# The first mixer's eight leading products, copied out of their banks ahead of the norm's factor

## The chip, the core and the metric

One program on one core of a Trainium2 chip. The metric is the device time of one execution in microseconds (us); the median of several runs is compared. TensorE (PE) multiplies, VectorE (DVE), ScalarE (ACT) and GpSimd (POOL) work on vectors, and SyncE (SP) and ACT issue DMAs.

## What is computed

Two transformer-like blocks, one behind the other, on 512 tokens of width 1024 in fp32. The change lies in the first block's mixer:

```python
u = rms_norm(h, mix_pre_g[l])
proj = u @ w_in[l]
(q_a, k_a, v_a, q_i, k_i, w_i, gate_b, gate_c, conv_in,
 g_a, g_b) = jnp.split(proj, split_points, axis=-1)
...
y_a = dsa_attention(q_a, k_a, v_a, q_i, k_i, w_i) @ w_a_out[l]
z = short_conv_causal(gate_c * conv_in, conv_w[l])
y_b = (gate_b * z) @ w_b_out[l]
merged = jax.nn.sigmoid(g_a) * y_a + jax.nn.sigmoid(g_b) * y_b
h = h + rms_norm(merged @ w_out[l], mix_post_g[l])
```

Ahead of it, `q_a`, `k_a`, `q_i` and `k_i` are rotated (rope). `dsa_attention` is sparse: an indexer sums relu(q_i . k_i) over eight heads with weights w_i into a score for each pair of tokens, a top-k of the scores picks the keys of each query, and the softmax runs over these alone. Memory cross-attention and a gated feed-forward end the first block; the second has a mixer with two attentions, a feed-forward and a gated addition.

## The kernel before

Features lie on the 128 partitions, tokens along the free dimension. A product takes eight slices of the 1024 inputs; each slice is three matmuls of halves in fp32r (`mm3`, L284 to L294), so a product of 128 outputs is 24 matmuls of 512 tokens, or 24 of 256 for half of the tokens (halves A and B). A weight is loaded raw by SP, cast on ACT (L252) and its rest taken on DVE (L253); two raw buffers and five cast pairs take turns.

The norm's factor is a number for each token, so a product can start on the gained input and be multiplied by the factor afterwards. `begin` (L316) uses this: it starts a stage's leading products by halves while the stage before it is still being normed and added. A half's steps come in lists: `post` (the factor of the stage before), `body` (adding, squares L563, the new input and its rest L513 and L514) and `norm` (sums on PE L582, root on DVE, the factor spread by PE L593 and copied by ACT L598). One step is issued behind each product, and what is to be done with a product (`put`) follows once its half's factor is known, which is what keeps the product in its PSUM bank until then. Weights for these products lie in buffers of the kinds that `K['lead:mix']` names (u and b are buffers of activations, w a regular pair).

There are five banks for products: three of the kind `lg`, two of the kind `mm`, taken in turn by a running count (`pm`); once `attending` is set only `mm` is taken, and the count runs on. Small buffers have eight slots (`t`), large ones 32 (`b`).

In the mixer, five leading products are the indexer's key (kk, which also holds the attention's key) and its four query tiles (qi0 to qi3). Their `put` is the rope: four ACT instructions (L785) fetch swapped quarters from the bank into y, DVE multiplies the bank by the cosine into x (L787), POOL multiplies y by the sine (L790), DVE adds (L791). The tables of cosine and sine are scaled by the factor on POOL first (L946). Values and head weights (vw, multiplied by the factor at L930) follow as a product of all tokens by `stream`. Then key and query tiles are split into halves of heads (L802, L803, L812 to L815), 24 pairs of indexer logits run (L823, L824) with a relu on ACT (L980) and a sum on DVE (L981) each, beside them the four query products of the attention (QA); 48 rounds of top-k on DVE (L992, L993), with the twelve convolution products and the first gates on PE beside them; and the attention, whose softmax begins at L833. A convolution step multiplies two products, c and ci, and three taps on them. Every engine works its own list in order; the list follows from the program's order through a scheduling layer, which lets engines run ahead of each other within the limits of buffers.

Of the kernel before, what the change touches and what calls it, by code (L numbers as in the profile page):

```python
# [15 lines left out]
OP = mybir.AluOpType  # L16
# [34 lines left out]
T_KK, T_QI, T_VW, T_QA, T_CONV, T_GB, T_GA = 0, 1, 5, 6, 10, 22, 30  # L51
# [35 lines left out]
 'urg:mixsh': 1,  # L87
 'sq:mixsh': 'PV',
 'bf:mix': [0, 1, 4, 6],
 'lead:mix': 'ubbbb',  # L90
 'ahead:mix': 5,
 'late:mix': [5, 0],
 'urg:crosssf': 1,
# [85 lines left out]
class Net:  # L179
# [123 lines left out]
    def begin(self, jobs, step, fill=()):  # L303


        first, second = step(A), step(B)
        wts = []
        for (w, n, xs, k0, _), tag in zip(jobs, K["lead:" + self.phase]):
            wts.append(self.lead_weights(w, n, len(xs), k0, tag) if tag != "w" else self.weights(w, n, len(xs), k0)[0])
        todo = first["post"] + first["body"] + first["norm"][:1]  # L310
        for go in self.rest:
            if todo:
                todo.pop(0)()
            go()
        self.rest = []
        for do in todo:  # L316
            do()
        todo = (second["post"][:2] + first["norm"][1:2] + second["post"][2:] + first["norm"][2:]
                + second["body"] + second["norm"])

        def advance():
            if todo:
                todo.pop(0)()

        for go in fill:
            go()
            advance()
        for _ in range(3):
            advance()

        for tok, d in zip(HALVES, (first, second)):
            waiting = []
            for (_, _, xs, _, put), wt in zip(jobs, wts):
                waiting.append((put, self.lin(wt, xs, tok)))
                advance()
                if not any(do in todo for do in d["norm"]):
                    while waiting:
                        put, ps = waiting.pop(0)
                        put(ps, tok)
            while any(do in todo for do in d["norm"]):  # L340
                advance()
            for put, ps in waiting:
                put(ps, tok)
        for do in todo:
            do()
# [428 lines left out]
    def rotated(self, w, n, xs, cos, sin, g=None, squares=None):  # L774

        nc = self.nc
        x, y = self.tmp(), self.tmp()

        def put(ps, tok):
            if squares is not None:  # L780
                nc.scalar.activation(squares[:, tok], ps, AF.Square)

            for b in range(4):
                src = slice(32 * (b ^ 1), 32 * (b ^ 1) + 32)
                nc.scalar.activation(y[32 * b : 32 * b + 32, tok], ps[src], AF.Copy, scale=1.0 if g is None else g[src])  # L785
            if g is None:
                nc.vector.tensor_tensor(x[:, tok], ps, cos[:, tok], op=OP.mult)  # L787
            else:
                nc.vector.scalar_tensor_tensor(x[:, tok], ps, g, cos[:, tok], op0=OP.mult, op1=OP.mult)
            nc.gpsimd.tensor_tensor(y[:, tok], y[:, tok], sin[:, tok], op=OP.mult)  # L790
            (nc.gpsimd if self.spared and K["F1"] else nc.vector).tensor_tensor(x[:, tok], x[:, tok], y[:, tok], op=OP.add)  # L791

        return x, (w, n, xs, 0, put)

    def heads(self, x):
# [123 lines left out]
    def projection(self, w, n, xs, r, alloc=None, light=False):  # L919

        nc = self.nc
        t = (alloc or self.tmp)((P, S), F32)

        def put(ps, tok):
            if light:
                nc.scalar.copy(t[:, tok], ps)  # L926
                if r is not None:
                    nc.gpsimd.tensor_tensor(t[:, tok], t[:, tok], r[:, tok], op=OP.mult)  # L928
            else:
                nc.vector.tensor_tensor(t[:, tok], ps, r[:, tok], op=OP.mult)  # L930

        return t, (w, n, xs, 0, put)

    def project(self, *args, **kw):
# [4 lines left out]
    def mix(self):  # L939
        self.phase = "mix"  # L940
        nc, h = self.nc, self.h
        cos, sin, cm = self.table("cos1"), self.table("sin1"), self.table("causal")

        def more(tok, r, rs):
            for t in (cos, sin):
# [2 lines left out]
        xs, r, step = self.enter("mix_pre_g", more)  # L948
        w = "w_in"
        turns = [self.rotated(w, n, xs, cos, sin) for n in (T_KK, T_QI, T_QI + 1, T_QI + 2, T_QI + 3)]  # L950
        vw, last = self.projection(w, T_VW, xs, r)
        self.begin([j for _, j in turns], step)
        self.stream([last])
        self.attending = True
        kk = turns[0][0]
        ka, ki = self.keys(kk, 0), self.keys(kk, 1)
# [5 lines left out]
        for j in range(NT):  # L962
            ps = self.pa()
# [5 lines left out]
        first = self.cp.tile([P, P], F32, tag="first", name="first")  # L969
# [3 lines left out]
        for i in range(1, NT):  # L973
            n = (i + 1) * P
            sc = self.big((P, n), F32)
            for hd in range(H):
                ps = self.bank("lg")
                self.logits(ps, qi[hd], hd % 2, i, ki, n)
                t = self.tmp((P, n))
# [5 lines left out]
        for t in range(4):  # L985
            x, job = self.rotated(w, T_QA + t, xs, cos, sin)
# [13 lines left out]
        rr = self.rowtile()  # L1000
        nc.gpsimd.tensor_tensor(rr, r, r, op=OP.mult)
        for j in range(4):
            c = self.project(w, T_CONV + 3 * j, xs, None, light=True)
            ci = self.project(w, T_CONV + 3 * j + 1, xs, None, light=True)
            nc.gpsimd.tensor_tensor(c, c, ci, op=OP.mult)
            nc.gpsimd.tensor_tensor(c, c, rr, op=OP.mult)
            tap = [self.gains[:, G_CONV + 3 * j + d : G_CONV + 3 * j + d + 1] for d in range(3)]
            z = self.tmp()
            nc.scalar.activation(z, c, AF.Copy, scale=tap[2])
            for d in (1, 0):  # L1010
                s = 2 - d
                nc.vector.scalar_tensor_tensor(z[:, s:], c[:, : S - s], tap[d], z[:, s:], op0=OP.mult, op1=OP.add)
            b = self.project(w, T_CONV + 3 * j + 2, xs, r, light=True)
            nc.gpsimd.tensor_tensor(b, b, z, op=OP.mult)
            bz.append(self.split(b, self.pair()))
# [618 lines left out]
```

## Time and profile before

| what | value |
|---|---|
| median of 3 runs | 2095.18 us (2094.7 to 2096.39) |
| the profiled execution, its own time | 2091.38 us |
| its span | 2089.6 us |
| mean granted clock of PE | 0.99 |
| busy: PE, DVE, ACT, POOL | 2011.4, 1544.4, 1101.7, 254.4 us |

The span is the time from the first instruction to the last in the profile; 1.8 us of the execution lie around it. The profiled execution is 3.8 us under the median. In the rows further down, a timeline's line gives the start, the busy time, engine and line, and what the instruction writes and reads; in square brackets stands how long the engine was idle before and what it waited for. Times are from the start of the span. A granted clock of 1.00 is 2.4 GHz, 0.50 is 1.2 GHz.

### The profile page before, as it was taken

Reading aid. Unit: us, or ns where it says so; the run is one execution under the profiler, and the core shown is the slowest. Engines: PE = TensorE matmul, PEld = TensorE weight load, DVE = VectorE, ACT = ScalarE, POOL = GpSimd, SP = SyncE. Lnnn points to the kernel's source line nnn. Section 1 sums busy time; section 2 is a strip of 40 time slices with the busy share of each in tenths; the row PEclk is TensorE's granted clock in tenths of the full one; section 3 lists DMA queues with packets and bytes.
Section 4 is the critical chain, followed back from the end, with each engine's and each line's share of the span. In section 5 each row is a group of like instructions: output and inputs, shape, how many; then the busy total and the mean of one; then the engine's idle time right before and its main releaser. Section 6 shows DMA issues by size and latency. Waiting matters only on the chain. (4 is left out here: it accounts for less than half of the span.)

```text
span 2089.6 us, 32337 instructions
## 1 busy us (share of the span) xinstructions
PE 2011.4 (96%) x12428; PEld 1766.1 (85%) x12428; DVE 1544.4 (74%) x2956; ACT 1101.7 (53%) x2052; POOL 254.4 (12%) x239
## 2 busy tenths in 40 slices
PE   8999999899999999999999998998999999999997
PEld 7899998778778888998999998776778888988997
DVE  7977786799775585587777869588987678666755
ACT  5644454673573454554445445467864436444752
POOL 2000002313331310040000003213100000000001
PEclk9999999899999999999999999999999999999999
DMA  5233333212222233221333342211112313323331
GB/s 163 91 112 97 106 107 122 71 61 91 91 71 95 77 120 103 93 70 51 113 110 102 106 141 72 66 41 51 41 41 81 114 31 122 99 89 104 112 101 41
DMA packets 66010, 186.43 MB, mean 89 GB/s; under 512 B 6976, under 2 KB 14144, under 8 KB 65856
## 3 DMA queue, kind: packets, MB, share of 16 engines
q1 hardware_dynamic: 63376, 180.97, 26.8%
q10 hardware_dynamic: 2448, 3.41, 0.5%
q8 instruction: 97, 1.59, 0.3%
q14 instruction: 57, 0.47, 0.1%
q0 software_dynamic: 32, 0.00, 0.0%
HBM read 182.25 MB, written 2.10 MB: 88 GB/s over the span
## 5 line engine op out<-in xcount | busy, mean ns | idle before, releaser
L290 PE MATMUL mm<-x,w 128*128 128x512 f32 (+1 forms) x2064 | 473.8, 379 | 0.0
L290 PE MATMUL mm<-b,w 128*128 128x256 f32 (+1 forms) x2625 | 448.6, 322 | 2.0 <-ACT b L510 1.8
L290 PEld LDWEIGHTS mm<-x,w 128*128 128x128 f32 x2064 | 364.0, 188 | 74.9 <-DVE v L1274 0.7
L290 PEld LDWEIGHTS mm<-b,w 128*128 128x128 f32 x2625 | 375.2, 188 | 48.9 <-ACT b L510 4.2
L252 ACT CAST w<-r 128x1024 fp32r<-128x1024 f32 (+2 forms) x256 | 229.8, 898 | 277.8 <-PE mm L290 118.0
L290 PE MATMUL lg<-x,w 128*128 128x256 f32 (+1 forms) x2460 | 348.6, 295 | 6.8 <-DVE t L1385 4.7
L253 DVE TENSOR_TENSOR w<-r,w 128x1024 fp32r<-128x1024 f32 (+2 forms) x254 | 267.8, 1055 | 116.3 <-ACT w L252 111.3
L290 PE MATMUL lg<-b,w 128*128 128x256 f32 (+1 forms) x1929 | 352.9, 334 | 0.0
L290 PEld LDWEIGHTS lg<-x,w 128*128 128x128 f32 x2460 | 315.9, 188 | 27.9 <-DVE t L1385 6.4
L290 PEld LDWEIGHTS lg<-b,w 128*128 128x128 f32 x1929 | 294.5, 188 | 42.1
L457 ACT CAST w<-r 128x1024 fp32r<-128x1024 f32 x147 | 154.6, 1053 | 138.1 <-PE lg L290 81.3
L458 DVE TENSOR_TENSOR w<-r,w 128x1024 fp32r<-128x1024 f32 x147 | 178.7, 1221 | 19.9 <-ACT w L457 19.4
L290 PE MATMUL mm<-x,u 128*128 128x256 f32 x756 | 108.1, 287 | 15.6 <-ACT x L513 7.1
L510 ACT CAST b<-t 128x512 fp32r<-128x512 f32 (+1 forms) x113 | 60.8, 539 | 112.5 <-DVE t L745 34.3
L290 PEld LDWEIGHTS mm<-x,u 128*128 128x128 f32 x756 | 96.9, 193 | 18.7 <-ACT x L513 7.5
L569 POOL TENSOR_TENSOR sh<-sh,sh 128x256 f32<-128x256 f32 x45 | 37.5, 834 | 502.8 <-ACT sh L563 499.9
L511 DVE TENSOR_TENSOR b<-t,b 128x512 fp32r<-128x512 f32 (+1 forms) x113 | 67.2, 596 | 26.3 <-ACT b L510 26.0
L569 POOL TENSOR_TENSOR sf<-sf,sf 128x256 f32<-128x256 f32 x28 | 23.3, 833 | 450.4 <-ACT sf L563 440.4
L563 ACT ACTIVATE sh<-h 128x256 f32<-128x256 f32 x128 | 49.9, 411 | 52.5 <-DVE h L630 22.7
L928 POOL TENSOR_TENSOR b<-b,rows 128x512 f32<-128x512 f32 x32 | 52.5, 1642 | 174.7 <-ACT b L926 174.7
L861 DVE TENSOR_TENSOR u<-tt,u 128x512 fp32r<-128x512 f32 x92 | 62.0, 684 | 9.9 <-ACT u L860 9.3
L290 PE MATMUL lg<-x,b 128*128 128x256 f32 x456 | 68.1, 291 | 0.0
(271 smaller groups left out, 2738.9 us busy)
## 6 DMA issues: line engine op xcount, KB each, us to landing
r<-in_ffn_w SPq DMA_DIRECT2D x86, 512.0 KB, 3.3
r<-in_w_in SPq DMA_DIRECT2D x64, 512.0 KB, 3.2
r<-in_ffn_w SPq DMA_DIRECT2D x68, 256.0 KB, 2.7
r<-in_w_up SPq DMA_DIRECT2D x32, 512.0 KB, 3.2
r<-in_w_down SPq DMA_DIRECT2D x32, 384.0 KB, 3.4
r<-in_ffn_w SPq DMA_DIRECT2D x16, 384.0 KB, 3.3
r<-in_w_out SPq DMA_DIRECT2D x8, 512.0 KB, 3.2
r<-in_xattn_w_k SPq DMA_DIRECT2D x8, 512.0 KB, 3.2
```

The lines of the kernel that those rows point to most:

```text
L252: nc.scalar.copy(hi, raw)
L253: self.second.tensor_tensor(lo, raw, hi.bitcast(F32), op=OP.subtract)
L290: self.nc.tensor.matmul(ps, lhsT=lhsT, rhs=rhs, start=start, stop=stop, skip_group_check=on)
L457: nc.scalar.copy(hi, raw)
L458: nc.vector.tensor_tensor(lo, raw, hi.bitcast(F32), op=OP.subtract)
L510: nc.scalar.copy(hi, src)
L511: nc.vector.tensor_tensor(lo, src, hi.bitcast(F32), op=OP.subtract)
L563: nc.scalar.activation(t, x, AF.Square)
L569: eng.tensor_tensor(ts[0], ts[0], t, op=OP.add)
L861: nc.vector.tensor_tensor(lo, ps[:, :n], hi.bitcast(F32), op=OP.subtract)
L928: nc.gpsimd.tensor_tensor(t[:, tok], t[:, tok], r[:, tok], op=OP.mult)
```

## The change

Eight products lead instead of five: vw and the first convolution step's c and ci join kk and qi0 to qi3, by halves. The result of each leaves its bank by an ACT copy that is issued right behind the product, ahead of the factor; what needs the factor (rope, vw times the factor) then works in the buffer that was copied to. vw no longer runs as one product of all tokens, and the first convolution step uses what was led. The mask's load (`causal`) is issued behind `begin` instead of ahead of it.

```diff
@@ -87,7 +87,7 @@
  'urg:mixsh': 1,
  'sq:mixsh': 'PV',
  'bf:mix': [0, 1, 4, 6],
- 'lead:mix': 'ubbbb',
+ 'lead:mix': 'ubbbwwbw',
  'ahead:mix': 5,
  'late:mix': [5, 0],
  'urg:crosssf': 1,
@@ -331,7 +331,11 @@
         for tok, d in zip(HALVES, (first, second)):
             waiting = []
             for (_, _, xs, _, put), wt in zip(jobs, wts):
-                waiting.append((put, self.lin(wt, xs, tok)))
+                ps = self.lin(wt, xs, tok)
+                first, then = getattr(put, "steps", (None, put))
+                if first is not None:
+                    first(ps, tok)
+                waiting.append((then, ps))
                 advance()
                 if not any(do in todo for do in d["norm"]):
                     while waiting:
@@ -790,6 +794,9 @@
             nc.gpsimd.tensor_tensor(y[:, tok], y[:, tok], sin[:, tok], op=OP.mult)
             (nc.gpsimd if self.spared and K["F1"] else nc.vector).tensor_tensor(x[:, tok], x[:, tok], y[:, tok], op=OP.add)
 
+        if squares is None and g is None:
+
+            put.steps = (lambda ps, tok: nc.scalar.copy(x[:, tok], ps)), (lambda ps, tok: put(x[:, tok], tok))
         return x, (w, n, xs, 0, put)
 
     def heads(self, x):
@@ -929,6 +936,12 @@
             else:
                 nc.vector.tensor_tensor(t[:, tok], ps, r[:, tok], op=OP.mult)
 
+        def then(ps, tok):
+            if r is not None:
+                (nc.gpsimd if light else nc.vector).tensor_tensor(t[:, tok], t[:, tok], r[:, tok], op=OP.mult)
+
+        if self.phase == "mix":
+            put.steps = (lambda ps, tok: nc.scalar.copy(t[:, tok], ps)), then
         return t, (w, n, xs, 0, put)
 
     def project(self, *args, **kw):
@@ -939,7 +952,7 @@
     def mix(self):
         self.phase = "mix"
         nc, h = self.nc, self.h
-        cos, sin, cm = self.table("cos1"), self.table("sin1"), self.table("causal")
+        cos, sin = self.table("cos1"), self.table("sin1")
 
         def more(tok, r, rs):
             for t in (cos, sin):
@@ -949,8 +962,10 @@
         w = "w_in"
         turns = [self.rotated(w, n, xs, cos, sin) for n in (T_KK, T_QI, T_QI + 1, T_QI + 2, T_QI + 3)]
         vw, last = self.projection(w, T_VW, xs, r)
-        self.begin([j for _, j in turns], step)
-        self.stream([last])
+
+        conv = [self.projection(w, T_CONV + d, xs, None, lambda shape, dt: self.big(shape, dt), True) for d in range(2)]
+        self.begin([j for _, j in turns] + [last] + [j for _, j in conv], step)
+        cm = self.table("causal")
         self.attending = True
         kk = turns[0][0]
         ka, ki = self.keys(kk, 0), self.keys(kk, 1)
@@ -1000,8 +1015,7 @@
         rr = self.rowtile()
         nc.gpsimd.tensor_tensor(rr, r, r, op=OP.mult)
         for j in range(4):
-            c = self.project(w, T_CONV + 3 * j, xs, None, light=True)
-            ci = self.project(w, T_CONV + 3 * j + 1, xs, None, light=True)
+            c, ci = (conv[d][0] if j == 0 else self.project(w, T_CONV + 3 * j + d, xs, None, light=True) for d in range(2))
             nc.gpsimd.tensor_tensor(c, c, ci, op=OP.mult)
             nc.gpsimd.tensor_tensor(c, c, rr, op=OP.mult)
             tap = [self.gains[:, G_CONV + 3 * j + d : G_CONV + 3 * j + d + 1] for d in range(3)]
```

What it moves, at three places. Line numbers behind the change are 4 to 15 higher. First, PE between half A and half B of the leading products. Before, the last of half A is qi3 (lg_4502), and kk's half B (mm_4551) and qi0's (lg_4589) follow:

```order
L290 MATMUL lg_4502<-x_3989,b_4052 128x256
L290 MATMUL lg_4502<-x_3991,b_4051 128x256
L290 MATMUL lg_4502<-x_3992,b_4051 128x256
L290 MATMUL lg_4502<-x_3991,b_4052 128x256
L290 MATMUL mm_4551<-x_3977,u_4007 128x256
L290 MATMUL lg_4589<-x_3977,b_4017 128x256
L290 MATMUL mm_4551<-x_3978,u_4007 128x256
```

With the change, the eighth product (ci, mm_4633) ends half A. The sum of squares for half B (L586) stands inside it, and kk's half B (lg_4659) follows:

```order
L290 MATMUL mm_4633<-x_3985,w_4068 128x256
L290 MATMUL mm_4633<-x_3986,w_4068 128x256
L586 MATMUL tt_4550<-ones,sh_4503 128x1
L586 MATMUL tt_4550<-ones,sh_4509 128x1
L586 MATMUL tt_4550<-ones,sh_4503 128x1
L586 MATMUL tt_4550<-ones,sh_4509 128x1
L290 MATMUL mm_4633<-x_3985,w_4069 128x256
L290 MATMUL mm_4633<-x_3987,w_4068 128x256
L290 MATMUL mm_4633<-x_3988,w_4068 128x256
L290 MATMUL mm_4633<-x_3987,w_4069 128x256
L290 MATMUL mm_4633<-x_3989,w_4068 128x256
L290 MATMUL mm_4633<-x_3990,w_4068 128x256
```

Half B's sums have moved from inside half B's products into the end of half A's, and what lies between the halves is three products longer. mm_4633 takes the bank of qi2 (mm_4469).

Second, ACT ahead of the first relu. Before, eight casts of the query halves (L802) stand right ahead of it:

```order
L802 CAST b_4767<-t_3998 64x512
L802 CAST b_4770<-t_3998 64x512
L802 CAST b_4773<-t_4000 64x512
L802 CAST b_4776<-t_4000 64x512
L802 CAST b_4779<-t_4002 64x512
L802 CAST b_4782<-t_4002 64x512
L980 ACTIVATE t_4816<-lg_4813 128x256
L980 ACTIVATE t_4822<-lg_4819 128x256
```

With the change (the casts are L809, the relu is L995, L944 copies c's and ci's half B, L922 casts values):

```order
L809 CAST b_4929<-t_3998 64x512
L809 CAST b_4932<-t_3998 64x512
L809 CAST b_4935<-t_4000 64x512
L809 CAST b_4938<-t_4000 64x512
L252 CAST w_5210<-r_5209 128x1024
L944 COPY b_4003<-lg_4851 128x256
L252 CAST w_5256<-r_5255 128x1024
L944 COPY b_4004<-mm_4877 128x256
L922 CAST v_4944<-tt_4942 128x64
L922 CAST v_4950<-tt_4948 128x64
L995 ACTIVATE t_4972<-lg_4969 128x256
```

Behind the last cast, two weight casts and two copies now stand ahead of the relus, and the last copy waits for ci's half B (mm_4877).

Third, DVE at the end of the top-k. Before, four of the top-k's instructions lie between the last two weight rests (L253), and the softmax follows:

```order
L253 TENSOR_TENSOR w_6013<-r_6011,w_6012 128x1024
L993 MATCH_REPLACE b_4910<-m_5283,b_4910 128x512
L992 MAX m_5286<-b_4910 128x8
L993 MATCH_REPLACE b_4910<-m_5286,b_4910 128x512
L994 TENSOR_SCALAR b_4910<-b_4910 128x512
L253 TENSOR_TENSOR w_6215<-r_6213,w_6214 128x1024
L833 ISA t_5882,sm_m_5883<-lg_5879,first 128x128
```

With the change (L1007 to L1009 are the top-k), the last weight rest but one stands earlier:

```order
L1007 MAX m_5424<-b_5066 128x8
L1008 MATCH_REPLACE b_5066<-m_5424,b_5066 128x512
L1007 MAX m_5427<-b_5066 128x8
L253 TENSOR_TENSOR w_6103<-r_6101,w_6102 128x1024
L1008 MATCH_REPLACE b_5066<-m_5427,b_5066 128x512
L1007 MAX m_5430<-b_5066 128x8
L1008 MATCH_REPLACE b_5066<-m_5430,b_5066 128x512
L1007 MAX m_5433<-b_5066 128x8
```

Behind this piece seven more rows like these follow, then the top-k's last instruction (L1009), the last weight rest (w_6305) and the softmax.

## Rows read from the trace of the kernel before

**Rows 1.** The page, part 1: busy time, share of the span and instructions

```profile
PE 2011.4 (96%) x12428; PEld 1766.1 (85%) x12428; DVE 1544.4 (74%) x2956; ACT 1101.7 (53%) x2052; POOL 254.4 (12%) x239
```

**Rows 2.** PE's waits, 360 to 430: us in total, times, longest

```profile
PE mm L290 <- DVE t L787: 4.4, 1, 4.4
```

**Rows 3.** PE's timeline: start, us, instruction, count, [idle before, releaser]

```profile
388.15 0.55 PE L290 MATMUL mm<-x,u 128*128 128x256 f32 x1 [4.43 <-DVE t L787]
...
409.02 5.77 PE L290 MATMUL lg<-x,w 128*128 128x512 f32 x24
417.47 0.39 PE L823 MATMUL lg<-b,b 128*128 128x256 f32 x1 [2.69 <-DVE b L803]
...
540.63 0.28 PE L823 MATMUL lg<-b,b 128*128 128x256 f32 x1
...
543.45 0.38 PE L823 MATMUL lg<-b,b 128*128 128x256 f32 x1 [1.95 <-DVE sm_m L833]
```

**Rows 4.** Busy time by stretch: PE, PEld, DVE, ACT, POOL, clock, DMA, GB/s

```profile
385.00:390.00 5.00, 1.58 (x6) 1.32 (x7) 4.12 (x8) 2.81 (x8) 3.46 (x6) 0.57 0.00 0
390.00:395.00 5.00, 4.03 (x17) 3.44 (x17) 5.00 (x10) 3.59 (x8) 2.25 (x3) 0.50 0.00 0
...
415.00:420.00 5.00, 1.93 (x8) 1.21 (x8) 4.78 (x8) 4.81 (x9) 0.00 (x0) 1.00 0.01 2
...
404.00:434.00 30.00, 26.29 (x141) 21.50 (x140) 25.36 (x52) 25.26 (x58) 7.20 (x9) 1.00 0.11 36
434.00:540.00 106.00, 106.00 (x456) 85.32 (x455) 101.75 (x199) 46.77 (x67) 33.99 (x23) 1.00 0.27 89
```

**Rows 5.** DVE's timeline, from the first score to the first softmax

```profile
425.16 9.12 DVE L981 SCALAR_TENSOR_TENSOR b<-t,wi,b 128x256 f32<-128x256 f32 x18
...
534.02 2.32 DVE L253 TENSOR_TENSOR w<-r,w 128x1024 fp32r<-128x1024 f32 x1
...
538.56 0.43 DVE L994 TENSOR_SCALAR b<-b 128x512 f32<-128x512 f32 x1
541.96 1.23 DVE L253 TENSOR_TENSOR w<-r,w 128x1024 fp32r<-128x1024 f32 x1 [2.98 <-ACT w L252]
543.10 0.28 DVE L833 CUSTOM_DVE_ANT_0 t<-lg,first 128x128 f32<-128x128 f32 x1
```

**Rows 6.** ACT's timeline, from the second factor's row on

```profile
404.33 0.37 ACT L598 COPY rows<-tt 128x256 f32<-128x256 f32 x1
...
412.62 1.54 ACT L785 ACTIVATE t<-mm 32x256 f32<-32x256 f32 x4
...
415.46 5.11 ACT L802 CAST b<-t 64x512 fp32r<-64x512 f32 x8
420.60 0.66 ACT L980 ACTIVATE t<-lg 128x256 f32<-128x256 f32 x2
...
422.34 1.05 ACT L252 CAST w<-r 128x1024 fp32r<-128x1024 f32 x1
```

**Rows 7.** DVE's groups by shape, 425 to 539: count, busy us, mean ns

```profile
L253 DVE TENSOR_TENSOR w<-r,w 128x1024 fp32r<-128x1024 f32 x17 | 25.0, 1469 | 0.0
L992 DVE MAX8 m<-b 128x8 f32<-128x512 f32 x16 | 11.0, 690 | 0.3
...
L916 DVE TENSOR_TENSOR v<-tt,v 128x64 fp32r<-128x64 f32 x1 | 0.2, 215 | 0.0
```

**Rows 8.** PE's timeline in the second block's mixer

```profile
1284.97 3.14 PE L290 MATMUL mm<-x,b 128*128 128x256 f32 x24 [2.35 <-DVE t L930]
```

**Rows 9.** Timelines of DVE and of POOL in the first half's ropes

```profile
385.88 0.93 DVE L791 TENSOR_TENSOR t<-t,t 128x256 f32<-128x256 f32 x1 [1.30 <-POOL t L790]
...
387.60 0.41 DVE L787 TENSOR_TENSOR t<-mm,b 128x256 f32<-128x256 f32 x1
...
388.32 0.41 DVE L791 TENSOR_TENSOR t<-t,t 128x256 f32<-128x256 f32 x1
...
386.49 0.90 POOL L790 TENSOR_TENSOR t<-t,b 128x256 f32<-128x256 f32 x1
```

## The prediction

> **What bounds the kernel now.** I read the page first. TensorE (PE) is busy 96% of the span [rows 1], so a gain must come out of the 78 us in which PE stands still, or out of work taken from it; the change takes none away, it computes the same products in another place. Next I read which waits PE has in the first mixer: the longest of the stage's start is 4.4 us, a matmul that waits for the rope's x·cos (L787), which reads a product's bank and so keeps it taken [rows 2]. PE's timeline puts it at 383.72 to 388.15, between the first-half and the second-half products of `begin`; a second stop of 2.69 us follows before the indexer's logits, at 417.47, and a third of 1.95 us at 543.45, where attention waits for its first softmax [rows 3]. These are the only places where less waiting in this stage could show, 9.1 us together.
>
> The windows then say what lies between the second stop and the third. From 434 to 540 PE is busy all 106.00 us with 456 matmuls, 0.2325 us each, and VectorE (DVE) 101.75 of the same 106 [rows 4]. Two engines are full side by side, and the third stop says which one ends last: PE is through its six first logits and waits, DVE is late. DVE's own timeline shows why: from the first score (L981) at 425.16 it works through the scores and 48 rounds of top-k to 538.99, stands 2.98 us for a weight cast, does one subtraction (L253) and comes to the first softmax at 543.10 [rows 5]. So the end of this stage is set by a DVE chain that starts at the first score. **A change of PE's order in front of it pays only if it brings that first score earlier or shortens that chain.**
>
> **What the change does to the stage, part by part.**
>
> *The stop of 4.43 us.* It goes in its old form: on ACT the first-half copies of kk and qi0 now stand ahead of the factor's row, and qi1's right behind it. But PE then needs another bank, and it stops at the eighth first-half product (the conv gate's) instead: its bank comes free by the copy of product four (qi2), which stands on ScalarE (ACT) behind the second half's squares and casts. I place this stop at about 389 to 394, five to six us, as long as the old one. Two products (qi3 and vw) are not copied early at all: their tiles use slots that kk and qi0 still hold, so they leave their banks only after the second factor. This costs or gains nothing by itself, because what follows waits for ACT.
>
> *ACT after the second factor.* Here is the main cost. Before, ACT ends the copy of the factor's row at 404.70 and reaches the first relu at 420.60 [rows 6], 15.9 us later. In between stand 15 swaps of 0.385 us (four take 1.54) and 12 casts of 0.64 (eight take 5.11) [rows 6], 13.5 us, so 2.4 us are waits. After the change there stand 24 swaps, the same 12 casts, nine copies of half a product at 0.37 (a bank-to-buffer copy of that size [rows 6]) and two weight casts at 1.05 (the row at 422.34): 9.2 + 7.7 + 3.3 + 2.1 = 22.3 us, and with the same waits 24.7. The first relu then comes at 404.70 + 24.7 = 429.4 instead of 420.60. Before, the first score came 4.6 us behind its relu, because DVE had casts of its own to do; that slack is used up: with 0.7 us from a relu's start to its score, the first score falls at 430.1, **4.9 us later** than 425.16. Bounds: without any wait on ACT 427.7 (2.5 later); with the factor itself 1.2 us later, because one weight subtraction (about 1.2 us alone [rows 5]) now stands inside its chain on DVE, 431.3 (6.1 later).
>
> *DVE from the first score to the last top-k round.* The instructions are the same but for one L253 fewer at 1.47 us on average, and four small ones more of 0.215 or less [rows 7]: **-0.7 us**.
>
> *The weight that is late at the end.* Before, the subtraction that frees the raw buffer ends at 536.34, and the next one can start 5.6 us after that, at 541.96 [rows 5]. After the change twelve instructions of the top-k (a MAX8 takes 0.690 us, a replacement about the same [rows 7]) lie between the two, some 8 us, so load and cast are through when the chain gets there: **-3.0 us**; if the load is late for another reason, 0.
>
> *PE towards attention.* The two conv products of 24 full matmuls leave the full stretch, 48 x 0.2325 = 11.2 us, while the relus that pace the logits come 8.8 us later. PE reaches attention at 540.63 + 8.8 - 11.2 = 538.2 or so. DVE reaches its first softmax at 543.10 + 4.9 - 0.7 - 3.0 = 544.3, **1.2 us later than before** (bounds -1.2 and +5.4). The products that were taken from a full PE are thus given back as a longer stop of about 5 us at the third place, where six logits still fit in.
>
> *The clock at that stop.* After the old stop of 4.43 us the granted clock was 0.57 and 0.50 in the next two stretches of 5 us, the 1.2 GHz level, and it stayed at 1.00 around the stop of 2.69 us [rows 4]. From 388.15 to about 395 at half speed PE loses some 3.4 us. The new stop lies between or above those two, so the price is 0 to 3.4; I take the middle, **+1.7**.
>
> *Later stages.* Both kernels take banks of two kinds in turn, and the number of products up to the end of the mixer changes from 13 to 16 where it counts, an odd step. So every later stage starts on the other kind. There are three banks of the one and two of the other: five leading products fit if they start on the first kind. In the second block's mixer the kernel before starts on the wrong one and waits 2.35 us for its fifth bank [rows 8]; that wait can go, unless the norm's chain behind it, which shows stops of its own, takes it up: 0 to -2.35, I take **-1.2**. Other stages turn the wrong way, but their first bank is freed before the fifth product starts; nothing is charged for them.
>
> *The rope from the buffer.* x·cos and the vw product with the factor now read two buffers instead of a bank and a buffer. A bank-reading x·cos took 0.41 us at 387.60; the rope's sum, which reads two buffers, took 0.93 at 385.88, while a GpSimd product (386.49, L790) ran, and 0.41 at 388.32 without one [rows 9]. For the ten half-products of the rope the price lies between 0 and 10 x (0.93 - 0.41) = 5.2 us. I take 0, as most of them run while DVE waits for ACT. The Trainium skill, page "SBUF — State Buffer", section "Who interferes with whom", says that a DVE instruction with two buffer inputs contends with a GpSimd instruction that reads the buffer, and one with a single such input does not; by that rule the move is bad, and my sum would be up to 5.2 us higher. The trace agrees with the rule as far as the two sums of 0.93 and 0.41 us go.
>
> *The mask's load.* It moves from ahead of the stage onto ACT's queue, behind the copy of the eighth product's first half, at about 395 by the stop above. On GpSimd a copy of the mask now stands ahead of the tables' scaling for the second half (L946), which can begin at about 405. A weight's load with its cast took under 5.6 us at the end of the stage [rows 5], so the mask is there in time: nothing. If that product ends later, the scaling and all ropes behind it wait; that lies within the 1.2 us of the upper bound.
>
> **Sum.** +1.2 (first score +4.9, work -0.7, late weight -3.0) +1.7 (clock) -1.2 (second mixer) = +1.7 us. The profiled execution took 2091.38 us, so 2093.1; the median of the runs shown is 2095.18, 3.8 above it, so **2096.9**. A measurement of this kernel tells about 0.2% from no change, 4.2 us. The forecast is: no difference that can be told.
>
> **The rivals.**
>
> *Faster: ACT is not the bound.* If the copies overtake in practice, or the relus are issued while the casts' data are still to come, the first score stays near 425.16. Then DVE's chain loses 0.7 and 3.0, PE's 11.2 us are more than enough to be there in time, and with the second mixer's 2.35 the kernel gains 6.1: 2089.1. For it speaks that ACT was busy only 25.26 of 30 us from 404 to 434 [rows 4]; against it that each engine works its list in order and the relus stand behind all copies and casts. Chance 0.22.
>
> *Slower: two-buffer ropes beside GpSimd.* If the x·cos of the second half run beside GpSimd's products (it does as many as DVE, 0.9 us each [rows 9]), DVE is late with the keys and query casts by up to 5.2 us, and since the end is DVE's chain, all of it counts: 2096.9 + 5.2 = 2102.1. It decides from the point where DVE, not ACT, ends last before the first score. Against it: DVE has slack there of 4.6 us now. Chance 0.15.
>
> *Slower: the clock.* If the stop in front of attention brings the full 3.4 us and the second mixer gives nothing: +1.2 + 3.4 = +4.6, 2099.8. It decides from a stop a little over 2.69 us. Chance 0.15.
>
> *The change does not free the banks.* Partly so, as said: two of the first half's eight products leave their banks only behind the second factor. It is in the forecast, since PE is not what ends last.
>
> **How the numbers follow.** The forecast has 0.48, with its own bounds at -1.2 - 2.35 = -3.5 and +5.4 + 3.4 = +8.8; most of it, 0.38, lies within 4.2 us, 0.08 above, 0.02 below. Rival one adds 0.20 to faster and 0.02 to same; rival two 0.15 to slower; rival three halves. Faster 0.22, same 0.47, slower 0.31. The range reaches from a little below rival one (2087.5) to a little above rival two (2103.5).
>
> **What would show it.** In the profile after: no 4.4 us for L787 but a stop of five us or so within the conv gate's first half; first relu at about 429 and first score at about 430; no idle before the last L253; first softmax at about 544; PE's stop there some 5 us long. The forecast is wrong if the first score stays near 425 or comes after 432, if PE and not DVE is last into attention, or if the stages behind it move by more than 3 us.

## The result, and the profile after

The changed kernel takes 2110.39 us (median of 5 runs, 2107.89 to 2113.48) beside 2095.18 us before (5 runs), a ratio of 1.0063 with an interval of 1.0046 to 1.0079. It is slower: by 15 us between these medians, by 13 by the ratio. I had forecast 2096.9 and no difference, with 2103.5 as the upper end. The profiled execution took 2110.39 us, its span is 2108.6.

Views of the profile show where it went. First PE's waits from 330 to 560, to be held against [rows 2, 3]:

```profile
PE mm L290 <- ACT t L799: 5.8, 1, 5.8
PE lg L830 <- DVE sm_m L840: 5.7, 1, 5.7
PE lg L830 <- ACT b L944: 3.5, 1, 3.5
PE tt L979 <- DVE wi L981: 3.4, 1, 3.4
```

The stop for the rope is gone; one of 5.8 us for the copy of qi2 has come, as expected, and the stop ahead of attention has grown from 1.95 to 5.7. Two stops of 3.5 and 3.4 among the first logits stand where 2.69 us stood ahead of them. PE's timeline has their places (start, us, instruction, idle before):

```profile
397.55 2.71 PE L290 MATMUL mm<-x,w 128*128 128x256 f32 x11 [5.85 <-ACT t L799]
...
432.77 0.39 PE L830 MATMUL lg<-b,b 128*128 128x256 f32 x1 [3.49 <-ACT b L944]
...
437.14 0.35 PE L979 MATMUL tt<-ident,t 72*128 72x72 f32 x1 [3.40 <-DVE wi L981]
...
555.75 0.58 PE L830 MATMUL lg<-b,b 128*128 128x256 f32 x1 [5.72 <-DVE sm_m L840]
```

ACT's timeline, for [rows 6]: the second factor's row, then the last casts, two weight casts, the copies of c and ci, and the first relus.

```profile
408.33 0.38 ACT L602 COPY rows<-tt 128x256 f32<-128x256 f32 x1
...
428.84 2.54 ACT L809 CAST b<-t 64x512 fp32r<-64x512 f32 x4
431.40 1.04 ACT L252 CAST w<-r 128x1024 fp32r<-128x1024 f32 x1
432.35 0.37 ACT L944 COPY b<-lg 128x256 f32<-128x256 f32 x1
432.62 1.05 ACT L252 CAST w<-r 128x1024 fp32r<-128x1024 f32 x1
433.57 0.37 ACT L944 COPY b<-mm 128x256 f32<-128x256 f32 x1
433.83 0.34 ACT L922 CAST v<-tt 128x64 fp32r<-128x64 f32 x2
434.04 0.96 ACT L995 ACTIVATE t<-lg 128x256 f32<-128x256 f32 x3
```

DVE's timeline, for [rows 5]: two weight rests ahead of the first score (one of 1.23 us and, from 434.50, one of 2.29), and the end of the top-k.

```profile
433.36 3.43 DVE L253 TENSOR_TENSOR w<-r,w 128x1024 fp32r<-128x1024 f32 x2
436.71 0.21 DVE L923 TENSOR_TENSOR v<-tt,v 128x64 fp32r<-128x64 f32 x1
...
437.30 0.90 DVE L996 SCALAR_TENSOR_TENSOR b<-t,wi,b 128x256 f32<-128x256 f32 x1
...
552.86 0.43 DVE L1009 TENSOR_SCALAR b<-b 128x512 f32<-128x512 f32 x1
553.20 2.29 DVE L253 TENSOR_TENSOR w<-r,w 128x1024 fp32r<-128x1024 f32 x1
555.41 0.28 DVE L840 CUSTOM_DVE_ANT_0 t<-lg,first 128x128 f32<-128x128 f32 x1
```

Beside the second of these rests GpSimd multiplied c and ci (its timeline, after):

```profile
434.01 1.70 POOL L1019 TENSOR_TENSOR b<-b,b 128x512 f32<-128x512 f32 x1 [5.19 <-ACT b L944]
435.79 2.13 POOL L1020 TENSOR_TENSOR b<-b,rows 128x512 f32<-128x512 f32 x1
```

In the kernel before, one rest stood there, with nothing beside it (DVE's timeline, before):

```profile
423.62 1.22 DVE L253 TENSOR_TENSOR w<-r,w 128x1024 fp32r<-128x1024 f32 x1
```

And the stretches around the stops, columns as in [rows 4]; the granted clock is the third figure from the end:

```profile
435.00:440.00 5.00, 2.86 (x13) 2.79 (x14) 4.61 (x13) 1.92 (x7) 2.84 (x2) 0.50 0.63 211
440.00:445.00 5.00, 5.00 (x20) 4.42 (x19) 4.47 (x9) 3.37 (x8) 0.00 (x0) 0.67 0.32 108
...
555.00:560.00 5.00, 4.25 (x12) 3.49 (x13) 3.94 (x21) 2.40 (x9) 0.68 (x1) 0.56 0.51 138
```

The first softmax has moved from 543.10 to 555.41, 12.3 us. PE began the last product of the stage before at 359.02 before and at 361.46 after, so 2.4 of them were there already, and the mixer itself takes 9.9 us more to its first softmax. The table cuts that way at five events, in the profiled executions; each figure is the difference of two starts in the timelines. "Behind" is from the first softmax to a weight cast (L252) in the middle of attention: the 79th of that line, at 624.39 before; in e5, which has one such cast more, the 80th.

| kernel | last product to factor's row | to first relu | to first score | to end of top-k (L994) | to first softmax | together | behind |
|---|---|---|---|---|---|---|---|
| before | 45.3 | 16.3 | 4.6 | 113.4 | 4.5 | 184.1 | 81.3 |
| before, second execution (e12) | 45.5 | 16.3 | 4.6 | 112.6 | 3.4 | 182.3 | 81.3 |
| e3: before, banks turned | 45.5 | 16.3 | 4.6 | 113.2 | 4.8 | 184.3 | 81.3 |
| after | 46.9 | 25.7 | 3.3 | 115.6 | 2.6 | 193.9 | 83.2 |
| after, banks turned (e4) | 44.7 | 25.7 | 3.3 | 114.2 | 2.6 | 190.5 | 85.1 |
| e1: five, copies | 44.6 | 19.4 | 2.8 | 117.4 | 2.7 | 186.9 | 81.3 |
| e2: eight, no copies | 44.3 | 24.6 | 1.7 | 111.7 | 2.0 | 184.3 | 84.7 |
| e2, second execution (e11) | 45.0 | 24.5 | 2.9 | 111.0 | 2.1 | 185.5 | 83.6 |
| e5: six, copies | 47.1 | 20.9 | 4.5 | 114.9 | 1.5 | 188.9 | 81.3 |
| e7: after, rests on GpSimd | 47.7 | 27.2 | 2.0 | 114.8 | 2.6 | 194.3 | 83.4 |
| e9: after, filled at attention | 47.1 | 25.8 | 3.3 | 115.3 | 3.7 | 195.1 | 81.3 |
| e13: e2, rests on GpSimd | 45.0 | 24.5 | 0.6 | 110.8 | 9.2 | 190.1 | 81.7 |
| e14: before, rests on GpSimd | 44.6 | 16.3 | 3.1 | 107.2 | 22.9 | 194.1 | 81.3 |

### The profile page after: what moved, and what is told of

The parts are those of the page before. It is cut to its first block, busy times and chain, and to the rows that moved or that the text cites. A ratio compares the mean times of both kernels' runs of the same rounds, so it can differ in the third digit from the quotient of the medians.

```text
span 2108.6 us, 32492 instructions
## 1 busy us (share of the span) xinstructions
PE 2022.4 (96%) x12500; PEld 1778.7 (84%) x12500; DVE 1548.3 (73%) x2957; ACT 1107.9 (53%) x2066; POOL 258.2 (12%) x239
## 5 line engine op out<-in xcount | busy, mean ns | idle before, releaser
L290 PE MATMUL mm<-x,w 128*128 128x512 f32 (+1 forms) x2184 | 490.0, 375 | 5.9 <-ACT t L799 5.8
L290 PEld LDWEIGHTS mm<-x,w 128*128 128x128 f32 x2184 | 380.4, 190 | 81.6 <-ACT t L799 6.0
L290 PE MATMUL mm<-b,w 128*128 128x256 f32 (+1 forms) x2553 | 434.3, 322 | 1.0 <-ACT b L514 0.9
L290 PEld LDWEIGHTS mm<-b,w 128*128 128x128 f32 x2553 | 366.8, 188 | 44.8 <-ACT b L514 1.9
L252 ACT CAST w<-r 128x1024 fp32r<-128x1024 f32 (+2 forms) x256 | 229.7, 898 | 281.6 <-PE mm L290 110.9
L290 PE MATMUL lg<-b,w 128*128 128x256 f32 (+1 forms) x2001 | 368.1, 334 | 0.9 <-ACT b L514 0.9
L253 DVE TENSOR_TENSOR w<-r,w 128x1024 fp32r<-128x1024 f32 (+2 forms) x254 | 270.0, 1064 | 113.9 <-ACT w L252 109.5
L290 PE MATMUL lg<-x,w 128*128 128x256 f32 (+1 forms) x2412 | 339.1, 293 | 5.3 <-DVE t L1399 3.7
L290 PEld LDWEIGHTS lg<-b,w 128*128 128x128 f32 x2001 | 303.2, 188 | 45.6 <-ACT b L514 2.3
L290 PEld LDWEIGHTS lg<-x,w 128*128 128x128 f32 x2412 | 308.2, 188 | 24.1 <-DVE t L1399 5.4
L290 PE MATMUL mm<-x,u 128*128 128x256 f32 x732 | 102.3, 288 | 10.3 <-ACT x L517 7.7
L515 DVE TENSOR_TENSOR b<-t,b 128x512 fp32r<-128x512 f32 (+1 forms) x113 | 67.2, 596 | 26.2 <-ACT b L514 25.8
```

The lines of the kernel that those rows point to most:

```text
L252: nc.scalar.copy(hi, raw)
L253: self.second.tensor_tensor(lo, raw, hi.bitcast(F32), op=OP.subtract)
L290: self.nc.tensor.matmul(ps, lhsT=lhsT, rhs=rhs, start=start, stop=stop, skip_group_check=on)
L515: nc.vector.tensor_tensor(lo, src, hi.bitcast(F32), op=OP.subtract)
```

## The experiments

My theory from this profile: three more products in half A and a longer list on ScalarE make the first score late; VectorE's chain from there on ends last; PE's stops then lower the clock. Rivals: the copies (and the ropes from buffers) are the cost; banks in later stages are.

**Copies and number apart.** e1 is the changed kernel with five leading products:

```diff
- 'lead:mix': 'ubbbwwbw',
+ 'lead:mix': 'ubbbb',
...
-        self.begin([j for _, j in turns] + [last] + [j for _, j in conv], step)
+        self.begin([j for _, j in turns], step)
+        self.stream([last])
...
```

> Five leading products as before, but copied out of their banks ahead of the factor; vw and the first convolution step as before. Theory one (the longer half A delays the second factor, and the longer list on ScalarE the first relu): the factor's row stays near 404.3 us, the first relu comes later by the ten copies of 0.37 us, some 4 us, the first softmax by 1 to 4 us, and the time is 2096 to 2099 us. Rival (the copies and the ropes that read two buffers are the cost): most of the 12.3 us that the stage lost shows here, 2104 us or more.

2100.08 us, ratio 1.0015 (0.9999 to 1.0030). The relu comes 3.1 us later after the row (ten copies of 0.37 are 3.7), the stage takes 2.8 more. Nearer to the theory, 1 us above its range; the row itself stands at 410.78, not near 404.3, because the last product ahead of it began 7.2 us later than before. e2 has eight, and no early copies; its banks are also turned, which costs nothing that can be told (e3 and e4 below):

```diff
-                first, then = getattr(put, "steps", (None, put))
+                first, then = None, put
...
         self.attending = True
+        self.turn += 1
```

> Eight leading products, but each stays in its bank until its factor is known, as before; the running count of banks is set so that later stages take banks as in the kernel before. Theory one: half A is still three products longer, so the second factor is 3 to 4 us late, and the first softmax 8 to 11 us later than before; 2103 to 2107 us. Rival (the copies are the cost): the first softmax within 4 us of before, 2099 us or less.

2104.99 us, ratio 1.0035 (1.0022 to 1.0047): in the theory's range for the time, and outside it for the place. The second factor is not late (44.3), and the stage as a whole takes 184.3, no longer than before; the first softmax is 3.4 us later than before, which is the place that the rival gave, with a time that it did not. What comes instead is the list: without a single early copy the first relu still stands 24.6 us behind the row, because it stands behind ci's copy on ScalarE, and PE ends ci's second half only then:

```profile
426.70 2.99 PE L290 MATMUL mm<-x,w 128*128 128x256 f32 x24
```

```profile
429.61 1.06 ACT L252 CAST w<-r 128x1024 fp32r<-128x1024 f32 x1 [0.58 <-PE mm L290]
430.57 0.36 ACT L933 COPY b<-mm 128x256 f32<-128x256 f32 x1
430.83 0.32 ACT L922 CAST v<-tt 128x64 fp32r<-128x64 f32 x2
431.04 1.99 ACT L996 ACTIVATE t<-lg 128x256 f32<-128x256 f32 x6
```

(PE's and ACT's timelines of e2.) Two limits lie at nearly the same place: ScalarE's list with copies, PE's eight second halves without. VectorE makes the delay good (111.7 and 2.0), PE stands 4.7 us for it at attention, and the part behind takes 3.4 us more. Of the 7 us that the ratio stands for, this is about half; where the rest lies is not shown. A second execution of the same kernel (e11) was for the spread:

> A second look at eight leading products without early copies, for the spread between executions of one kernel: from the first softmax to the end within 4 us of the first look's 1557.5 us, and from the last product of the stage before to the first softmax within 1 us of 184.3 us.

185.5 us, 1.2 above the first and so 0.2 outside; from the first softmax to the end 1554.9 us, within 4.

**Banks in later stages.** e3 is the kernel before with the line `self.turn += 1` as above, e4 the changed kernel with it.

> The kernel before, with one more step of the running count of banks at the end of the leading products, so that all later stages start on the other kind of bank. Theory one (later stages lose by where the clock and the waits happen to fall): within 2 us of before, 2093 to 2097 us. Rival (banks in later stages cost the 6 us that the trace after shows behind the mixer): 2101 us.

> The changed kernel, with the running count of banks turned back, so that later stages start on the kind of bank that they had before. Theory one: 2108 to 2111 us, as the changed kernel. Rival (banks in later stages cost 6 us): 2104 us.

e3: 2097.53 us, 0.9994 (0.9980 to 1.0008). e4: 2110.40 us, 1.0059 (1.0036 to 1.0083). The banks cost nothing that can be told, either way; this rival fell.

**Six products.** e5 leads vw but not the convolution: `'lead:mix': 'ubbbww'`, and c and ci as before.

> The changed kernel with six leading products (vw joins, the convolution's two do not), all copied out early. Theory (the list on ScalarE between the second factor and the first relu, and the weight rests on VectorE ahead of the first score, set the loss): four copies of 0.37 us and the wait for the eighth product leave the list, so the relu comes 1.5 to 5 us sooner after the factor's row than the 25.7 us of the changed kernel, and no convolution product on GpSimd slows the weight rests; 2099 to 2105 us. Rival (the number of products in half A sets it): 2101 to 2103 us, in proportion to the one product of three that stays. Rival (copies alone): no difference to five with copies, 2100 us.

2103.95 us, 1.0042 (1.0028 to 1.0056). The relu is 20.9 us behind the row, 4.8 sooner, as the theory had it; the time is in the theory's range and 1 us above the proportion, so it hardly tells those apart. It speaks against the copies alone. The score came 4.5 us behind the relu, no sooner than before: VectorE's eight query subtractions, 5.7 us, stood there to the end.

**Small buffers.** e6: `'slots': [31, 10, 5]` for `[32, 8, 5]`.

> The changed kernel with ten small buffers instead of eight (and 31 large ones instead of 32), so that qi3's and vw's first halves need no buffer that kk and qi0 still hold, and all eight first halves can leave their banks ahead of the second factor. Theory: two copies move ahead of the factor's row, the list behind it is 0.7 to 1.5 us shorter, and the time 1 to 2 us less than the changed kernel's 2110 us. Rival (the held buffers cause the stops ahead of the logits): 4 us less or more.

2115.04 us, 1.0082 (1.0061 to 1.0104), a miss for both: the copies did move ahead and the list behind the row got 1.2 us shorter, but PE stood 8.7 us for the second half's squares (48.5 to the factor's row instead of 46.9). What the held buffers cost stays open.

**VectorE relieved.** e7 and e8 set `self.second = nc.gpsimd` around the attention's query products, in the changed kernel and in the one before.

> The changed kernel with the rests of the four attention query weights on GpSimd instead of VectorE. Theory (VectorE's chain from the first score to the last round of the top-k ends last, PE stands 5.7 us for it): VectorE is relieved of four rests of 1.2 to 1.7 us, two of them right ahead of the first score, so the first softmax comes 3 to 6 us sooner and the time is 2105 to 2107 us. Rival (PE or ScalarE ends last): 2109 us or more.

> The kernel before with the same move of four weight rests to GpSimd. Theory: VectorE's chain gets 3 to 5 us shorter, but PE is only 1.95 us ahead of it there, so 1 to 2 us are gained: 2094 us beside 2096. Rival (the move slows VectorE by as much as it takes away, since GpSimd shares its port to the buffer): no difference or slower.

2114.58 us (1.0079, 1.0052 to 1.0105) and 2101.45 us (1.0031, 1.0011 to 1.0050): the theory missed in both, and the times are those of the rivals. In e7 the two rests ahead of the first score were gone from VectorE, and the score still came 29.2 us behind the factor's row instead of 29.0: the relu was 1.5 us later, and the last four query subtractions (L810), beside the rests on GpSimd now, took 4.94 us instead of 2.84. PE still stood 5.3 us for VectorE at attention, so e7 does not speak for PE or ScalarE ending last. GpSimd's timeline of e8 shows what the move cost there: rests of 2.4 to 2.6 us stand among the norm's own steps, and the factor's row comes at 48.7 instead of 45.3.

```profile
387.21 2.45 POOL L629 TENSOR_TENSOR b<-b,rows 128x256 f32<-128x256 f32 x3
389.62 2.52 POOL L253 TENSOR_TENSOR w<-r,w 128x1024 fp32r<-128x1024 f32 x1
392.10 0.91 POOL L569 TENSOR_TENSOR sh<-sh,sh 128x256 f32<-128x256 f32 x1
```

So the convolution's rests were moved instead, which fall behind the norm: `'conv': 'P'` for `'V'`, in e2's kernel (e13) and in the one before (e14).

> Eight leading products without early copies, with the rests of the convolution's weights on GpSimd instead of VectorE, so that they fall into the top-k and behind the norm. Theory (VectorE's chain holds attention, and the stop there costs the clock behind it): ten rests of 1.47 us leave the chain, some of it is lost to the shared port; PE's stop of 4.7 us at attention shrinks to under 2 us, the clock stays at 1.00 behind it, from the first softmax to the middle of attention 81.3 us instead of 84.7, and 3 to 6 us less in all than the 2105 us of eight without copies. Rival (another engine holds attention): 2104 us or more.

> The kernel before with the same move of the convolution's weight rests to GpSimd. Theory: PE stands only 1.95 us for VectorE there, so at most 2 us are gained, 2094 us beside 2096; the stop goes. Rival (GpSimd's slower rests arrive late for PE): slower by 2 us or more.

2107.33 us (1.0053, 1.0033 to 1.0074) and 2105.29 us (1.0052, 1.0035 to 1.0069): the times are those of the rivals again. VectorE's chain did get shorter, from 113.4 and 112.6 to 107.2 us in e14 (in e13 hardly, to 110.8), and the stop for the softmax went; but the attention came later, because PE now ended last. Its waits from 440 to 560 in e14, and DVE's first softmax, which now waits for PE:

```profile
PE mm L290 <- DVE t L787: 6.4, 4, 2.6
PE mm L290 <- ACT t L926: 2.4, 2, 1.7
```

```profile
553.85 0.29 DVE L833 CUSTOM_DVE_ANT_0 t<-lg,first 128x128 f32<-128x128 f32 x1 [2.91 <-PE lg L824]
```

VectorE's chain is what holds attention in the kernels that keep these rests on it. These two runs do not show what a relief is worth by itself: in e14 PE came to attention 12.8 us later than before (553.41 against 540.63), after 8.8 us of waits that it did not have there, so the move to GpSimd made PE late as well. In e13 the part behind fell to 81.7 from 84.7, as expected of the clock.

**The clock behind the stops.** e9 puts 22 matmuls that nothing reads ahead of attention in the changed kernel (extra work):

```diff
+    def idle_matmuls(self, xs, count):
+        ps = self.bank("o")
+        for m in range(count):
+            x = xs[m % len(xs)]
+            self.nc.tensor.matmul(ps, lhsT=x[0][:, 0:P], rhs=x[0], start=m == 0, stop=m == count - 1)
...
+        self.idle_matmuls(xs, 22)
         def units():
```

> The changed kernel with 22 matmuls of 512 tokens more, 5.1 us, whose result nothing reads, on PE right ahead of attention, where it stands 5.7 us for VectorE. Theory (the stop itself costs nothing, but the half clock that follows it does): the stop shrinks to under 1.5 us, the granted clock stays at 1.00 behind it, and from the first softmax to the middle of attention the trace shows 1.5 to 3 us less than the changed kernel; the time falls by as much, to about 2108 us. Rival (PE is the bound there): 5 us are added, 2115 us.

The stop is 1.6 us, the clock behind it 1.00, the part behind 81.3 instead of 83.2, with 5.1 us of work added:

```profile
555.00:560.00 5.00, 3.43 (x19) 2.80 (x18) 4.79 (x21) 3.57 (x10) 0.53 (x2) 1.00 0.47 143
```

The time, 2109.64 us (1.0066, 1.0046 to 1.0086), cannot be told from the changed kernel's: 1.9 us are less than the runs resolve, and the mixer ahead took 1.2 more in this execution, in which a second weight rest stood ahead of the softmax. The other kernels say the same as e9: where PE's stop at attention was 2.0 us or less, or none (before, e12, e3, e1, e5, e9, e13, e14), the part behind took 81.3 to 81.7 us; where it was 4.4 to 5.7 us (after, e4, e7, e2, e11, and e6), 83.2 to 85.8. e10 puts 12 such matmuls behind the last leading product and 14 (on the last query tile) behind the third pair of logits:

> The changed kernel with 26 matmuls of 512 tokens more whose result nothing reads: 12 of them behind the last leading product, 14 behind the third pair of indexer logits, where PE stands 3.5 and 3.4 us. Theory (the half clock that follows these stops slows the logits, and so the scores): the clock stays near 1.00 through the logits and the first scores; from the first score to the end of the top-k 111 to 113 us instead of 115.6, and 2 to 4 us less in all, 2106 to 2108 us. Rival (the scores are paced by ScalarE and VectorE alone): no change there, 2110 us or more.

2114.51 us, 1.0091 (1.0067 to 1.0114): the filling pushed the relu to 30.8 us behind the row and made a stop of 5.1 us of its own (clock 0.65 and 0.67 behind it); from score to end 114.0. It does not tell the theories apart.

**The kernel before, again.**

> The kernel before, looked at a second time, for the spread between executions of one kernel. If the profiled execution of the kernel before was a quick one, as its 2091 us beside a median of 2095 us says, the part from the first softmax to the end is 1549 to 1552 us here instead of 1546.5, and the part from the last product of the stage before to the first softmax again 184 us. If the later stages really lost 6 us by the change, it is 1546 to 1547 us again.

1546.43 us from the softmax to the end, 182.3 ahead of it: I had expected the former to be longer. It is the figure that would speak for a loss of 6 us in the later stages; e3 speaks against that, whose later stages took 1551.2 us at the time of the kernel before. Both profiled executions of the kernel before (2091.38 and 2089.13 us) lie at the quick end of its timed runs, which reach from 2089.14 to 2104.4 us.

## Why the prediction was wrong

What failed is the path to the first score and the chain behind it. I had the first softmax 4.9 - 0.7 - 3.0 = 1.2 us later; it came 9.7 + 2.2 - 2.0 = 9.9 us later. Of the 8.7 us between, 2.9 are the chain's, 2.6 the way from the relu to its score, 1.6 the factor's row, 1.0 the late weight and 0.6 ScalarE's list. Point by point, after against before in the profiled executions:

- **The old stop of 4.43 us and its successor**: right. It came at 391.7 to 397.55 within ci's first half, 5.85 us long; in e4, with a stop of 5.97 us, the factor's row was no later than before (44.7), so the stop itself need not cost anything.
- **The mask's load, nothing**: right, but closely. It was issued at 404.79, not at 395, and GpSimd's copy of the mask (408.42 to 408.71) ended with the factor's row.
- **ACT after the second factor**: right in size. 25.7 us from the row's start to the first relu, 9.4 more than before; I had 24.7 from its end and 8.8 more. What I had not seen is that PE's second halves end at nearly the same point, so that the copies are not the only reason (e2: 24.6).
- **"With 0.7 us from a relu's start to its score": this is the step that failed first.** No row stood behind the 0.7, and it was 3.26. Two weight rests stand there on DVE, 1.23 and 2.29 us (the second beside GpSimd's products of the convolution's c and ci, which now come this early), and so do the head weights, for which the score waits. I had seen both weight casts in ACT's list and not followed their rests to DVE. That the rests alone make the delay is not shown: e7, which took them away, paid for it elsewhere. With the factor 1.6 us later in this execution (not in e4, -0.6), the first score was 9.7 us later, not 4.9, and at 437.30 behind the 432 that I had named as a sign of being wrong.
- **"The work -0.7"**: there was one rest fewer in the chain from the first score to the last top-k instruction, as I had it, and the chain took 2.2 us more all the same. I had left out waits: DVE stood 4.4 us in it, 1.1 before. PE had stood 3.5 and 3.4 us just ahead, the logits ran at a granted clock of 0.50 and 0.67, a relu waited for them and a score for the relu (the two rows behind this list). The kernels whose clock there fell to 0.50 to 0.55 in a stretch of 5 us (after, e1, e4, e7, e9) took 114.2 to 117.4 us for the chain; e2, e11 and e6, which kept 1.00 there, 111.0 to 111.7. The kernel before kept 1.00 too and took 112.6 to 113.4, with the one rest more. That goes together; the run that was to show the cause (e10) did not. e2 also shows what the chain is worth: its relu is nearly as late as the changed kernel's and its stage no longer than before, and 3.9 of the 9.6 us between the two lie in the chain.
- **"The late weight -3.0"**: the wait went, but the last rest took 2.29 us beside GpSimd's work instead of 1.23, so 2.0 were gained.
- **PE's stop of about 5 us at attention**: 5.72, but by luck. I had PE there at 538.2 and the softmax at 544.3; they came at 549.15 and 555.41, 2.4 of it from ahead of the mixer. Both ends were late by nearly the same.
- **The clock at attention, +1.7**: +1.9, and shown by e9 to follow the stop. The size was in part luck, the middle of 0 to 3.4: in other kernels stops of 4.4 to 5.3 us cost 2.1 to some 4.5.
- **The second mixer, -1.2**: the wait of 2.35 us went and others took its place; the part of the program around it took as long as before. e3 and e4 say the same: nothing.
- **The rope from the buffer, 0**: right for the sum. Seven of the ten took 0.41 to 0.43 us, three 0.95 to 0.98 where a GpSimd product ran, 1.6 us together, at places where DVE had waits behind it. The rule of the Trainium skill that I had set against it (page "SBUF — State Buffer", section "Who interferes with whom") says that a DVE instruction with two buffer inputs contends with a GpSimd instruction that reads the buffer. The trace agrees in these three and in the weight rests (1.23 and 2.29); the 5.2 us it could have cost did not come, since few ropes met a GpSimd product.

The relu that waits for the logits and the score that waits for the relu, in ACT's and DVE's timelines of the changed kernel:

```profile
443.61 2.61 ACT L995 ACTIVATE t<-lg 128x384 f32<-128x384 f32 x6 [1.39 <-PE lg L831]
```

```profile
447.04 5.52 DVE L996 SCALAR_TENSOR_TENSOR b<-t,wi,b 128x512 f32<-128x512 f32 x9 [1.22 <-ACT t L995]
```

The mixer to its first softmax and attention behind it thus give 9.9 + 1.9 = 11.8 us of the 13 to 15 that were timed; I had 1.2 + 1.7. Of the three rivals the one on the clock named a mechanism that was at work, but only at one of its two places, and none named VectorE's rests. The rest of the 19.0 us by which the two spans differ (2.4 ahead of the mixer, some 5 behind attention's middle) is not shown to come from the change: e3 has 2.6 ahead of the mixer and 4.7 behind the first softmax too, and its time is that of the kernel before. Against e3, the two spans differ by 11.5 us: -0.1 ahead of the mixer, 9.6 in it, 2.0 behind its first softmax. Why both profiled executions of the kernel before were quick there stays open.

## What to carry to other kernels

Taking work from a full engine pays only if the engine that ends last gets its first input no later: here the products that moved left PE 5.7 us early at a chain that VectorE had started 10 us late. Follow each moved weight through all its steps (load, cast, rest) to the queue where the critical chain begins; here two rests, 3.5 us together, stood where I had counted nothing. And a stop that is free on paper is to be charged with the clock that follows it, at every place where one comes.

## What was not expected of the hardware

A weight rest (128x1024, two buffers) took 1.23 us on VectorE alone and 2.29 beside GpSimd's work, and 2.4 to 3.0 on GpSimd itself; in e7 the subtractions that VectorE did beside such rests took 4.94 us for four instead of 2.84. Moving such work there slowed both.

The length of a stop did not settle the clock by itself: 2.69 us ahead of the logits left it at 1.00 in the kernel before, and in e14, at the same place and of the same length, it was 0.50 from 420 to 422.

Programs that are the same up to the mixer's logits reached its last product of the stage before at 359.0 and 358.6 us (before, twice) and at 361.6 (e3); the others reached it at 359.8 to 366.6. No run tells why.
